# A two-layer attention and retention encoder: pair 14 in seven products in the input projection, pair 15's second low part by ScalarE and an accumulating transfer

## The chip, the cores and the metric

One core of a Trainium2 chip runs the whole program. The metric is the device time of one execution in microseconds (us), the median of several runs. Engines: TensorE (PE; PEld is its weight loading), VectorE (DVE), ScalarE (ACT), GpSimd (POOL), SyncE (SP). SP and POOL issue the transfers (DMAs), each in the order of its own queue.

## The reference

Two layers (DEPTH = 2), 256 tokens, width 4096, all in float32:

```python
for l in range(DEPTH):
    h = rmsnorm(x, norm_w[l])
    proj = h @ w_in[l]                       # 4096 x 11264
    aq, ak, av, ag, rq, rk, rv, rg = jnp.split(proj, SPLIT_POINTS, axis=-1)
    ...                                      # per-head norms, axial rotary
    a_out = silu(ag) * gqa_attention(aq, ak, av)
    r = rmsnorm(bidirectional_retention(rq, rk, rv, log_gf, log_gb), ret_norm[l])
    r_out = silu(rg) * r
    x = x + jnp.concatenate([a_out, r_out], axis=-1) @ w_out[l]   # 4096 x 4096
return rmsnorm(x, final_norm)
```

The two projections are nearly all of the arithmetic. There are 16 attention heads in 4 groups and 8 retention heads in 4 pairs.

## The kernel before

**Phases and blocks.** There are four phases: w_in of layer 0, w_out of layer 0, w_in of layer 1, w_out of layer 1. An input phase has 11 blocks of 2 x 512 columns (BLOCKS, here one "block" is two pieces of the projection, such as `ag` group 0 with `aq` group 0), an output phase four. A block runs over the contraction of 4096 as 16 pairs of two 128-row tiles (NP = 16). So in a block each pair multiplies a 2 x 2 arrangement of tokens and contraction tiles with a 2 x 2 arrangement of contraction tiles and columns. That can be done in eight products of 512 columns (EIGHT_PRODUCTS, line 145) or, with sums of the blocks on both sides, in seven (SEVEN_PRODUCTS, line 134, the scheme of Strassen and Winograd). The two kinds can be mixed in one block, because both add into the same banks of PSUM, M1 to M7. When a block ends, `combining` (line 1690) copies M1 and adds the other banks into two pages, ca and cb.

**Precision.** A float32 operand is split into a high part, rounded to the matmul's fast float32 form (F32R), and a low part, the remainder. One product is three matmuls: high by high, low by high, high by low (`block`, line 1588; the records' names are `M<-whi,x7h` and so on: weights' part, tokens' part; x7 is an operand of a pair in seven products, x8 in eight, xm of a pair that has seven in one kind of phase and eight in the other).

**Weight pages.** Weights come by SP as pages of 512 KB (`wraw`, 128 x 1024 float32, RAWS = 6 slots).
- A pair in eight products has the pages A and B. For each, ScalarE makes the high part (`high`, line 680, a CAST `whi<-wraw`), VectorE the low part (`low`, line 701, `wlo<-wraw,whi`). HIGHS = 4 and LOWS = 3 buffers hold them until PE is done.
- A pair in seven products has four: A, T, B, U. VectorE first makes the sums T (`make_v`, line 623) and U in two halves (`make_u`, `end_u`, lines 634 and 642), each `wsum`. T and U then get a high and a low part like a full page; of B only one half is used (`whb`, `wlb`).
- The page B of some pairs in eight products is **far** (`fars`, line 164): ScalarE makes its high part (`fhi`) and its negated copy (`flo`, `far_parts` and `far_low`, lines 724 and 737), and a transfer by GpSimd's queue adds the weights from memory to that copy (`add`, line 742). VectorE does nothing for it. FAR = 2 buffers hold it, and the work starts FAR_LEAD = 10 us ahead.

Before, SEVEN_IN names the pairs 0, 2, ..., 12 for w_in, SEVEN_OUT 0, 2, ..., 14 for w_out (lines 156 and 157). FAR_IN and FAR_OUT are the odd pairs to 13 (lines 158 and 159). In the border blocks, the last of each input phase and the first of each phase but the very first, `fars` adds pairs in eight products up to BORDER_FAR = 10: before, pairs 14 and 15 in w_in and pair 15 in w_out. In the first block of all, pairs 0, 1, 4 and 5 (DIRECT) are multiplied without splitting, in four passes.

**Order of the work.** The program is written out by a planner: a small simulation with a clock per engine (`Clock`, line 228), a model of the transfers (`Transfers`, line 254) and slots for buffers. At each moment `pick` (line 879) chooses the next instruction of an engine: urgent steps first, then weight operations by their due place in PE's order (`best`, line 763, for VectorE among the next LOOK = 5 that are ready) against steps of tasks. Tasks are what lies between the projections: `in_task` (norms, rotary, gates), `attention_rest` (line 1356) with `attention_pair` (line 1278), `retention_weights`, `retention_pair` and `retention_values` (lines 1480 and 1496). They share PAGES = 8 pages of SBUF with the combining; `running` (line 850) lets a task begin when its `need` of pages is there, at most AT_ONCE = 3 at a time. What they yield is stored to memory, read back and split into operands for the next phase (`Turn`, line 1073; `split_pair`, line 947). All engines' queues run in the planned order.

All VectorE and ScalarE calls pass through line 249, all matmuls through line 1183 (`matmul`), all transfers through line 373 (`dma`); so the rows' lines tell little and their names tell the operation.

Of the kernel before, what the change touches and what calls it, by code (L numbers as in the profile page):

```python
# [12 lines left out]
F32R = mybir.dt.float32r  # L13
# [31 lines left out]
DUE_LEAD = 25.0  # L45
RUSH, SPLIT_LEAD = 2.8, 6.0
# [32 lines left out]
NEED = {"ak": 4, "ag": 3, "rk": 4, "rg": 6}  # L79
# [76 lines left out]
SEVEN_IN = (0,2,4,6,8,10,12)  # L156
SEVEN_OUT = (0, 2, 4, 6, 8, 10, 12, 14)
FAR_IN=(1,3,5,7,9,11,13)
# [69 lines left out]
class Clock:  # L228


    def __init__(self, engine, cost, lap, now):
        self._engine, self._cost, self._lap, self._now = engine, cost, lap, now
        self.until, self._wrote, self.calls = 0.0, None, 0
# [5 lines left out]
    def __getattr__(self, name):  # L239
        call = getattr(self._engine, name)  # L240

        def recorded(out, *args, **kwargs):
            self.until = max(self.until, self._now.t)
            if self._wrote and any(meet(self._wrote, extent(v)) for v in sources(args, kwargs)):
                self.until += self._lap + OWN_PASS
            self.until += self._cost(name, out, args, kwargs) - self._lap
            self._wrote = extent(out)
            self.calls += 1
            return call(out, *args, **kwargs)  # L249

        return recorded
# [96 lines left out]
def hybrid_encoder(  # L348
# [185 lines left out]
    class Weights:  # L534


        def __init__(self):
            self.pages, at = [], 0.0
            for phase in range(2 * DEPTH):
                w = w_out if phase % 2 else w_in  # L540
                for b in range(N_OUT2 if phase % 2 else N_IN):
                    start = (phase, b) == (0, 0)
                    end = (phase, b) == (2 * DEPTH - 1, N_OUT2 - 1)
                    for n, (p, k, uses) in enumerate(pages_in_order(phase, start, end)):
                        g = Page()
                        g.pair, g.kind, g.phase, g.uses = p, k, phase, uses
# [234 lines left out]
    class Lane:  # L781
# [4 lines left out]
        def __init__(self, steps, need=0, own=0, owner=None, after=0.0, hurry=True, due=1e9, start=lambda: True):  # L786
# [62 lines left out]

    def running():  # L850
# [89 lines left out]
    phase_now, need_at = [-1], {}  # L940
    for g in weights.pages:
        if not g.direct:
            need_at.setdefault((g.phase, g.pair), g.at)
    plain, plain_left = {}, list(DIRECT)
# [213 lines left out]
    def split_turned(parts, src):  # L1158

        to = [v.rearrange("p i (m a t) -> p m i a t", m=MT, t=BLK) for v in parts]  # L1160
        v = src.rearrange("p (a m i t) -> p m i a t", a=4, m=MT, t=BLK)
# [11 lines left out]
    def parts_of(name, shape):  # L1173
        return page(shape, name + "h", F32R), page(shape, name + "l", F32R)

# [102 lines left out]
    def attention_pair(g, h, kv, qT, rs, done):  # L1278
# [4 lines left out]
        for e in range(2):  # L1283
            s = (yield from take_bank()).rearrange("p (m k) -> p m k", m=MT)
            for m in range(MT):
                product(s[:, m, :], at(qT, ALL, h + e, slice(m * P, (m + 1) * P)), kT, True, True)
            if h and e:
                drop(2)
# [67 lines left out]
    def attention_rest(L, g):  # L1356
# [86 lines left out]
    def retention_head(wT, v, sg, e, L=None):  # L1443
        o = (yield from take_bank()).rearrange("p (m v) -> p m v", m=MT)
        for m in range(MT):
            for k in range(MT):
                product(
                    o[:, m, :],
                    at(wT, ALL, 2 * e + k, slice(m * P, (m + 1) * P)),
# [3 lines left out]
                )  # L1453
        yield "A"
# [5 lines left out]
        yield 1.0  # L1460
        yield "V"
        if L is not None:
# [5 lines left out]
            return  # L1468
# [9 lines left out]
        free_bank()  # L1478

    def retention_pair(L, i, gacc, vacc):  # L1480
# [4 lines left out]
        for e in range(2):  # L1485
            yield from retention_head(wT, v, gacc, e)
        drop(4)
# [8 lines left out]
    def retention_values(L, i, c, k):  # L1496
# [4 lines left out]
        for e in range(2):  # L1501
            yield from retention_head(wT, v, o, e, L)
        drop(4)
# [420 lines left out]
    def program():  # L1924
        nonlocal sums
        for l, L in enumerate(layers):
            for bi, (one, _) in enumerate(BLOCKS):
# [33 lines left out]
                if one[0] == "rk":  # L1961
                    for i in (2 * one[1], 2 * one[1] + 1):
# [3 lines left out]
                            need=3,  # L1966
                        )
                if one[0] == "ag":
# [4 lines left out]
                        need=6,  # L1973
# [91 lines left out]
```

## Time and profile before

| | us |
|---|---|
| median of 3 runs | 2584.72 (2584.64 to 2585.1) |
| span of the profiled execution, first to last instruction | 2581.7 |
| PE busy | 2565.6 |
| VectorE busy | 2302.2 |
| ScalarE busy | 1914.1 |
| GpSimd busy | 445.3 |

The page gives the profiled execution by its span; a device time of that one execution isn't listed, so the median stands beside it, 3.0 us longer. The granted TensorE clock was 0.998 on average. Busy shares are means over stages; what a stage waits for is read from the views of that stage. A block's end can be found in the trace by ScalarE's copy of M1 (`ca<-M`): the stretches below are cut there, for instance block 6 of layer 0's input phase from 502.2 to 588.1 us.

### The profile page before, as it was taken

Reading aid. Unit: us, or ns where it says so; the run is one execution under the profiler, and the core shown is the slowest. Engines: PE = TensorE matmul, PEld = TensorE weight load, DVE = VectorE, ACT = ScalarE, POOL = GpSimd, SP = SyncE. Lnnn points to the kernel's source line nnn. Section 1 sums busy time; section 2 is a strip of 40 time slices with the busy share of each in tenths; the row PEclk is TensorE's granted clock in tenths of the full one; section 3 lists DMA queues with packets and bytes.
Section 4 is the critical chain, followed back from the end, with each engine's and each line's share of the span. In section 5 each row is a group of like instructions: output and inputs, shape, how many; then the busy total and the mean of one; then the engine's idle time right before and its main releaser. Section 6 shows DMA issues by size and latency. Waiting matters only on the chain.

```text
span 2581.7 us, 34413 instructions
## 1 busy us (share of the span) xinstructions
PE 2565.6 (99%) x11474; PEld 2116.3 (82%) x11474; DVE 2302.2 (89%) x2912; ACT 1914.1 (74%) x2679; POOL 445.3 (17%) x595
## 2 busy tenths in 40 slices
PE   9999999999999999999999999999999999999998
PEld 5888888888888888888888888888888888888886
DVE  7898988998888899888998889989988888998887
ACT  7877776777777688767887776777778777876765
POOL 0022211221221210111212121212212211101110
PEclk9999999999999999999999999999999999999999
DMA  8999989998899899999999999989989998989996
GB/s 303 315 291 289 287 275 289 271 308 266 275 292 284 269 279 251 285 292 291 314 297 283 291 278 279 280 279 285 303 265 284 282 277 264 296 244 283 275 268 227
DMA packets 213107, 727.00 MB, mean 282 GB/s; under 512 B 25520, under 2 KB 32304, under 8 KB 212928
## 3 DMA queue, kind: packets, MB, share of 16 engines
q1 hardware_dynamic: 147616, 521.31, 57.3%
q0 software_dynamic: 65312, 203.49, 34.5%
q8 instruction: 90, 1.47, 0.2%
q14 instruction: 89, 0.73, 0.1%
HBM read 676.46 MB, written 48.23 MB: 281 GB/s over the span
## 4 chain that ended last, share of the span: by engine, by line
PE 95%; DVE 3%; issue 1%; DMA 1%; ACT 0%; POOL 0%; DVEq 0%; POOLq 0%; ACTq 0%
PE M L1183 92%; PE ps L1183 3%; DVE wlo L249 1%; DVE wsum L249 1%; DMA wraw<-in_w_in 0%; DMA flo<-in_w_in 0%; DVE x8l L249 0%; DVE cb L249 0%; PE ps L1022 0%; PE ps L2002 0%; DVE xf L249 0%; DVE x7l L249 0%; DVE ca L249 0%; ACT whi L249 0%; DVE wlb L249 0%
## 5 line engine op out<-in xcount | busy, mean ns | idle before, releaser
L249 ACT CAST whi<-wraw 128x1024 fp32r<-128x1024 f32 x522 | 541.8, 1045 | 176.6 <-PE M L1183 132.8
L249 DVE TENSOR_TENSOR wlo<-wraw,whi 128x1024 fp32r<-128x1024 f32 x522 | 633.1, 1214 | 40.2 <-issue 13.9
L249 DVE TENSOR_TENSOR wlo<-wsum,whi 128x1024 fp32r<-128x1024 f32 x432 | 526.0, 1218 | 132.2 <-PE M L1183 120.0
L249 ACT CAST whi<-wsum 128x1024 fp32r<-128x1024 f32 x432 | 453.4, 1050 | 194.9 <-PE M L1183 139.1
L1183 PE MATMUL M<-whi,x7h 128*128 128x512 f32 x1248 | 487.0, 390 | 0.0
L1183 PE MATMUL M<-whi,x7l 128*128 128x512 f32 x1248 | 485.9, 389 | 0.0
L1183 PE MATMUL M<-whi,x8h 128*128 128x512 f32 x1052 | 409.6, 389 | 0.0
L1183 PE MATMUL M<-whi,x8l 128*128 128x512 f32 x1052 | 409.4, 389 | 0.0
L1183 PE MATMUL M<-wlo,x7h 128*128 128x512 f32 x1248 | 386.1, 390 | 1.7 <-DVE wlo L249 1.5
L1183 PE MATMUL M<-fhi,x8h 128*128 128x512 f32 x836 | 325.7, 390 | 0.0
L1183 PE MATMUL M<-fhi,x8l 128*128 128x512 f32 x836 | 325.4, 389 | 0.0
L1183 PE MATMUL M<-wlo,x8h 128*128 128x512 f32 x1052 | 311.7, 390 | 1.4 <-DVE wlo L249 1.4
L373 POOL DMA_DIRECT2D flo<-in_w_in x156 | 138.4, 887 | 992.0 <-ACT flo L249 878.4
L249 ACT CAST fhi<-wraw 128x1024 fp32r<-128x1024 f32 (+1 forms) x214 | 223.4, 1044 | 110.3 <-PE M L1183 86.3
L249 DVE TENSOR_TENSOR wsum<-wraw 128x1024 f32<-128x1024 f32 x216 | 263.2, 1218 | 15.5 <-DMA wraw<-in_w_in 8.6
L1183 PEld LDWEIGHTS M<-wlo,x7h 128*128 128x128 f32 x1248 | 233.1, 188 | 50.8 <-DVE wlo L249 3.2
L1183 PEld LDWEIGHTS M<-whi,x7l 128*128 128x128 f32 x1248 | 234.4, 188 | 48.9 <-DVE wlo L249 0.2
L1183 PEld LDWEIGHTS M<-whi,x7h 128*128 128x128 f32 x1248 | 234.4, 188 | 48.6 <-issue 0.5
L249 ACT ACTIVATE flo<-fhi 128x1024 fp32r<-128x1024 f32 (+1 forms) x214 | 225.5, 1054 | 9.3 <-PE M L1183 2.4
L1183 PEld LDWEIGHTS M<-wlo,x8h 128*128 128x128 f32 x1052 | 196.8, 188 | 42.2 <-DVE wlo L249 1.9
L1183 PEld LDWEIGHTS M<-whi,x8l 128*128 128x128 f32 x1052 | 197.5, 188 | 41.0
L1183 PEld LDWEIGHTS M<-whi,x8h 128*128 128x128 f32 x1052 | 197.5, 188 | 40.8 <-ACT whi L249 0.3
(280 smaller groups left out, 3779.1 us busy)
## 6 DMA issues: line engine op xcount, KB each, us to landing
wraw<-in_w_in SPq DMA_DIRECT2D x703, 512.0 KB, 5.8
wraw<-in_w_out SPq DMA_DIRECT2D x256, 512.0 KB, 6.2
flo<-in_w_in POOLq DMA_DIRECT2D x156, 512.0 KB, 8.4
flo<-in_w_out POOLq DMA_DIRECT2D x54, 512.0 KB, 8.6
full<-next_dram POOLq DMA_DIRECT2D x18, 512.0 KB, 10.5
p_dram<-room POOLq DMA_DIRECT2D x64, 128.0 KB, 4.0
pT<-p_dram POOLq DMA_DIRECT2D x16, 512.0 KB, 10.8
next_dram<-room POOLq DMA_DIRECT2D x40, 128.0 KB, 5.1
```

What stands on the lines that cost most here:

```text
L249: return call(out, *args, **kwargs)
L373: getattr(nc, name).dma_start(to, src, **kw)
L1183: nc.tensor.matmul(out, a, b, start=start, stop=stop)
```

## The change

In w_in, pair 14 goes from eight to seven products, and page B of pair 15 becomes far in every block (so all eight odd pairs are). Pair 14 is then of the same kind in all phases (no xm operands any more).

The operands of the tasks are split in halves: attention's queries and retention's decayed scores are split two heads (or one head) at a time into one page that holds both parts, instead of all at once into two pages. A task of attention's rest then needs 5 pages (6 before), `rg` tasks 5 (6 before). In `retention_head` the second half is split between the first head's matmuls and its norm.

The planner's rules change too: attention's rest has a due time (REST_LEAD), a start condition by the time left to the next block's border (TAKES in place of `need == 3`), VectorE prefers weight operations that have been ready for SOFT = 0.4 us, the pause after the power function on GpSimd is planned as 1.7 us (1.0), and the clocks also count a lap where an instruction overwrites what the one before it read.

```diff
+REST_LEAD = 20.0
+POOL_REST = 1.7
+SOFT = 0.4
+TAKES = 65.0, 50.0
...
-NEED = {"ak": 4, "ag": 3, "rk": 4, "rg": 6}
+NEED = {"ak": 4, "ag": 3, "rk": 4, "rg": 5}
...
-SEVEN_IN = (0,2,4,6,8,10,12)
+SEVEN_IN = (0, 2, 4, 6, 8, 10, 12, 14)
...
-FAR_IN=(1,3,5,7,9,11,13)
+FAR_IN = (1, 3, 5, 7, 9, 11, 13, 15)
...
-            if self._wrote and any(meet(self._wrote, extent(v)) for v in sources(args, kwargs)):
+            if self._wrote and any(meet(self._wrote, extent(v)) for v in sources(args, kwargs)) or any(meet(v, extent(out)) for v in self._read):
...
-                ops = [o for o in self.ops["V"][:LOOK] if o.ready()]
+                at, ops = now.t, []
+                for rest in (SOFT, 0.0):
+                    now.t = at - rest
+                    ops = ops or [o for o in self.ops["V"][:LOOK] if o.ready()]
+                now.t = at
...
-                if held[0] + v.need - v.own + pledged(v) + (0 if v.own else 2 if v.need == 3 else wanted[0]) + spare() <= PAGES:
+                if held[0] + v.need - v.own + pledged(v) + (0 if v.own else 2 if v.takes > to_border() else wanted[0]) + spare() <= PAGES:
...
+    def parts_in_one(name):
+        v = page([P, 2, 2, SEQ], name, F32R)
+        return v[:, 0], v[:, 1]
...
-        qT = parts_of("aq", [P, 4, SEQ])
-        yield from split_turned(qT, q)
+        done = []
+        qT = parts_in_one("aq")
+        yield from split_turned(qT, q, 0, 2)
+        one = spawn(attention_pair(g, 0, kv, qT, rs, done))
+        qT = parts_in_one("aq")
+        yield from split_turned(qT, q, 2, 2)
         drop()
-        done = []
-        one = spawn(attention_pair(g, 0, kv, qT, rs, done))
...
-        wT = parts_of("wT", [P, 4, SEQ])
-        yield from split(wT, D.rearrange("p (k q) -> p k q", k=4))
+        D = D.rearrange("p (k q) -> p k q", k=4)
+        wT = parts_in_one("wT")
+        yield from split(wT, D[:, :2])
+        return D, wT
...
+        drop(3 if e else 1)
+        wT = None if e else (yield from second(D))
         yield "A"
...
-        yield 1.0
+        yield POOL_REST
...
-                        need=6,
+                        need=5,
+                        takes=TAKES[0],
+                        due=borders[min(bi + 3, N_IN)] - REST_LEAD,
```

## Rows read from the trace of the kernel before

**Rows 1.** The page's busy times: engine, busy us, share of the span, instructions.

```profile
span 2581.7 us, 34413 instructions
PE 2565.6 (99%) x11474; PEld 2116.3 (82%) x11474; DVE 2302.2 (89%) x2912; ACT 1914.1 (74%) x2679; POOL 445.3 (17%) x595
```

**Rows 2.** Three stretches: length; busy PE, PEld, DVE, ACT, POOL; clock, DMA, GB/s.

```profile
0.00:94.40 94.40, 90.92 (x329) 61.17 (x329) 77.14 (x136) 76.93 (x143) 5.20 (x10) 1.00 0.91 307
94.40:2555.30 2460.90, 2459.71 (x11081) 2043.01 (x11082) 2207.91 (x2747) 1827.08 (x2518) 439.01 (x583) 1.00 0.93 282
2555.30:2581.70 26.40, 14.99 (x67) 12.07 (x65) 17.17 (x32) 10.11 (x18) 1.13 (x2) 0.85 0.54 200
```

**Rows 3.** The chain that ended last: start us, length us, what.

```profile
1.49 4.45 PE ps L2002 x10
...
94.37 147.17 PE M L1183 x648
```

**Rows 4.** Whom PE waited for: us in total, times, longest.

```profile
PE M L1183 <- DVE wlo L249: 2.9, 3, 1.4
```

**Rows 5.** Whom VectorE waited for, the first row.

```profile
DVE wlo L249 <- PE M L1183: 132.4, 119, 2.7
```

**Rows 6.** Groups by shape: count, busy us, mean ns of one, idle before, releasers.

```profile
L249 DVE TENSOR_TENSOR wlo<-wraw,whi 128x1024 fp32r<-128x1024 f32 x518 | 630.4, 1219 | 40.2 <-issue 13.9 <-PE M L1183 12.3 <-ACT whi L249 9.3
L249 ACT CAST whi<-wraw 128x1024 fp32r<-128x1024 f32 x518 | 539.3, 1049 | 176.6 <-PE M L1183 132.8 <-DMA wraw<-in_w_in 20.1 <-DMA wraw<-in_w_out 16.8
L249 DVE TENSOR_TENSOR wlo<-wsum,whi 128x1024 fp32r<-128x1024 f32 x432 | 526.0, 1218 | 132.2 <-PE M L1183 120.0 <-ACT whi L249 3.7 <-ACT rkqh L249 3.1
...
L249 DVE TENSOR_TENSOR wsum<-wraw 128x1024 f32<-128x1024 f32 x216 | 263.2, 1218 | 15.5 <-DMA wraw<-in_w_in 8.6 <-DMA wraw<-in_w_out 6.1
...
L249 ACT ACTIVATE flo<-fhi 128x1024 fp32r<-128x1024 f32 x210 | 223.0, 1062 | 9.3 <-PE M L1183 2.4 <-ACT fhi L249 0.4
...
L249 DVE TENSOR_TENSOR wsum<-wsum,wraw 128x512 f32<-128x512 f32 x216 | 147.7, 684 | 1.0
...
L249 DVE TENSOR_TENSOR wlb<-wraw,whb 128x512 fp32r<-128x512 f32 x216 | 147.1, 681 | 19.7 <-ACT whb L249 19.7
L373 POOL DMA_DIRECT2D flo<-in_w_in x156 | 138.4, 887 | 992.0 <-ACT flo L249 878.4 <-ACT xmh L249 56.2 <-PE M L1183 47.7
L249 ACT CAST whb<-wraw 128x512 fp32r<-128x512 f32 x216 | 131.7, 610 | 56.7 <-PE M L1183 45.1 <-issue 11.4 <-ACT whi L249 0.2
```

**Rows 7.** The page's DMA issues: count, KB each, median us to landing.

```profile
flo<-in_w_in POOLq DMA_DIRECT2D x156, 512.0 KB, 8.4
```

**Rows 8.** Stretches, columns as in rows 2: an input phase, two blocks.

```profile
94.40:945.80 851.40, 851.40 (x3861) 708.54 (x3862) 765.59 (x954) 631.18 (x887) 167.44 (x227) 1.00 0.92 283
...
502.20:588.10 85.90, 85.90 (x382) 71.12 (x382) 79.98 (x94) 63.26 (x85) 20.68 (x28) 1.00 0.94 301
...
1201.40:1283.40 82.00, 82.00 (x363) 67.91 (x363) 80.08 (x114) 69.38 (x105) 16.98 (x24) 1.00 0.97 302
```

**Rows 9.** Stretches at the start and the borders, columns as in rows 2.

```profile
60.00:80.00 20.00, 19.86 (x88) 16.24 (x87) 19.93 (x32) 15.74 (x28) 0.85 (x1) 1.00 1.02 324
...
930.00:958.00 28.00, 28.00 (x137) 23.63 (x136) 23.20 (x39) 21.44 (x40) 5.28 (x7) 1.00 0.93 288
...
1320.00:1380.00 60.00, 60.00 (x273) 49.62 (x273) 52.05 (x75) 46.54 (x70) 7.93 (x9) 1.00 0.96 283
```

**Rows 10.** VectorE in order of time: start us, length us, what, idle before.

```profile
88.05 1.23 DVE L249 TENSOR_TENSOR wsum<-wraw 128x1024 f32<-128x1024 f32 x1 [2.78 <-DMA wraw<-in_w_in]
```

More of the change, by code (lines that the diff above doesn't have):

```diff
@@ L243, in recorded @@
             self.until = max(self.until, self._now.t)
-            if self._wrote and any(meet(self._wrote, extent(v)) for v in sources(args, kwargs)):
+            if self._wrote and any(meet(self._wrote, extent(v)) for v in sources(args, kwargs)) or any(meet(v, extent(out)) for v in self._read):
                 self.until += self._lap + OWN_PASS
             self.until += self._cost(name, out, args, kwargs) - self._lap
-            self._wrote = extent(out)
+            self._wrote, self._read = extent(out), [extent(v) for v in sources(args, kwargs)]
             self.calls += 1
@@ L545, in __init__ @@
                         g = Page()
-                        g.pair, g.kind, g.phase, g.uses = p, k, phase, uses
+                        g.pair, g.kind, g.phase, g.block, g.uses = p, k, phase, b, uses
                         g.direct = start and p in DIRECT
@@ L784, in hybrid_encoder, with __init__ @@
         pair = None
-        def __init__(self, steps, need=0, own=0, owner=None, after=0.0, hurry=True, due=1e9, start=lambda: True):
+        def __init__(self, steps, need=0, own=0, owner=None, after=0.0, hurry=True, due=1e9, takes=0.0, start=lambda: True):
+            self.takes = takes
             self.hurry, self.start, self.due = hurry, start, due
@@ L848, in pledge, with to_border @@
         current[0].need = n
+    def to_border():
+        at = weights.place()
+        return next((v - at for v in borders_at if v > at), 1e9)
     def running():
@@ L939, in hybrid_encoder @@
     version = [-1] * NP
-    phase_now, need_at = [-1], {}
+    phase_now, need_at, border = [-1], {}, {}
     for g in weights.pages:
+        border.setdefault((g.phase, g.block), g.at)
         if not g.direct:
             need_at.setdefault((g.phase, g.pair), g.at)
+    borders_at = sorted(border.values())
     plain, plain_left = {}, list(DIRECT)
@@ L1156, in later, with split_turned @@
         return lambda: landed(REST)
-    def split_turned(parts, src):
+    def split_turned(parts, src, h=0, n=4):
         to = [v.rearrange("p i (m a t) -> p m i a t", m=MT, t=BLK) for v in parts]
-        v = src.rearrange("p (a m i t) -> p m i a t", a=4, m=MT, t=BLK)
+        v = src.rearrange("p (a m i t) -> p m i a t", a=4, m=MT, t=BLK)[:, :, h : h + n]
         yield "A"
@@ L1285, in attention_pair @@
             for m in range(MT):
-                product(s[:, m, :], at(qT, ALL, h + e, slice(m * P, (m + 1) * P)), kT, True, True)
-            if h and e:
-                drop(2)
+                product(s[:, m, :], at(qT, ALL, e, slice(m * P, (m + 1) * P)), kT, True, True)
+            if e:
+                drop()
             yield "V"
@@ L1437, in decays, with second, retention_heads, retention_head @@
         yield lambda: landed(W_REST)
-        wT = parts_of("wT", [P, 4, SEQ])
-        yield from split(wT, D.rearrange("p (k q) -> p k q", k=4))
+        D = D.rearrange("p (k q) -> p k q", k=4)
+        wT = parts_in_one("wT")
+        yield from split(wT, D[:, :2])
+        return D, wT
+    def second(D):
+        wT = parts_in_one("wT")
+        yield from split(wT, D[:, 2:])
         drop()
         return wT
-    def retention_head(wT, v, sg, e, L=None):
+    def retention_heads(wT, v, sg, L=None):
+        D, wT = wT
+        for e in range(2):
+            wT = yield from retention_head(wT, v, sg, e, L, D)
+    def retention_head(wT, v, sg, e, L, D):
         o = (yield from take_bank()).rearrange("p (m v) -> p m v", m=MT)
@@ L1484, in retention_pair @@
         wT = yield from decays(i)
-        for e in range(2):
-            yield from retention_head(wT, v, gacc, e)
-        drop(4)
+        yield from retention_heads(wT, v, gacc)
         pledge(2)
@@ L1500, in retention_values @@
         o = page([P, MT, NB], "o")
-        for e in range(2):
-            yield from retention_head(wT, v, o, e, L)
-        drop(4)
+        yield from retention_heads(wT, v, o, L)
         L.pairs = i + 1
@@ L1926, in program @@
         for l, L in enumerate(layers):
+            borders = [border[2 * l, b] for b in range(N_IN)] + [border[2 * l + 1, 0]]
             for bi, (one, _) in enumerate(BLOCKS):
@@ L1966, in program @@
                             need=3,
+                            takes=TAKES[1],
                         )
```

7 lines of the change are left out of this document (4 added, 3 removed).

## The prediction

> **What bounds the kernel now.** I read the page's busy times first: TensorE (PE) is busy for 2565.6 of 2581.7 us, its weight loads for 82%, VectorE for 89%, ScalarE for 74% [rows 1]. Three stretches show where PE's idle 16 us lie: 3.5 before 94.4 us, 11.4 in the last 26.4 us, and 1.2 in the 2460.9 us between [rows 2]. A busy PE need not be a full one, so I turned to the chain of waits: one unbroken piece of it is 648 matmuls in 147.17 us, 0.2271 us each [rows 3], and of that length is every 512-column step. PE's list of waits holds, for the big products, three on VectorE, 2.9 us in all [rows 4]. VectorE, on the other hand, waits 132.4 us, 119 times, for PE to give back a buffer of low parts [rows 5]: it runs ahead, 1.1 us at a time. So from 94.4 us on each matmul that is taken out is worth its 0.227 us, as long as VectorE, now the second busiest, still delivers in time. That is the question.
>
> Here the Trainium skill speaks against it. Its page "Perfetto Trace Analysis", section "Identifying the Most-Contended Engine", says that matmul busy time doesn't tell how full TensorE is and that busy weight loads and the share of peak do; the engine with the highest occupancy is to be relieved first. By that reading PE would have 18% to spare and VectorE's 89% would be the most contended, and the change would load the wrong engine. What it would give is the last rival below. The 0.2271 us per matmul, without a gap over 147 us, doesn't agree with that reading.
>
> **What it removes.** Pair 14 takes seven products instead of eight in the 11 blocks of w_in of both layers. A product is three matmuls (high by high, low by high, high by low). 22 x 3 = 66 matmuls x 0.2271 us = 15.0 us, all on the path that sets the end. PE's matmul records should fall from 11474 to 11408.
>
> **What it adds on VectorE.** As eight products pair 14 needed two low parts, 2 x 1.219 = 2.44 us. As seven it needs low parts of A (1.219), of the two sums T and U (2 x 1.218) and of half of B (0.681), and the sums, 1.218 + 2 x 0.684 [rows 6]: 6.92 us. Difference +4.48. Pair 15's page B loses its low part on VectorE, -1.22. So +3.26 us in each of the 19 blocks where neither pair was far. In the three border blocks (the last block of each input phase, the first of layer 1) both pairs were far already, so that one low part of pair 14 was VectorE's: there it is 6.92 - 1.22 = +5.70, and pair 15 changes nothing. 19 x 3.26 + 3 x 5.70 = 79 us. The split operands cut 24 VectorE operations in two (per attention group two more, per retention pair one more, eight of each); a cut costs the fixed part, 2 x 0.684 - 1.218 = 0.15 us, 3.6 us in all. Pair 14's own operand, twice, some 0.7 us more each (four sums of 128 columns and a wider low part; an estimate from the same slope). Sum: 84 us, VectorE from 2302 to some 2386 us.
>
> **On ScalarE.** Pair 14: three full high parts and a half instead of two, 3 x 1.049 + 0.610 - 2 x 1.049 = +1.66; pair 15: one more pass, the negated copy, +1.06. 19 x 2.72, plus 3 x 0.60 at the borders, plus 24 cuts x 0.17 (2 x 0.610 - 1.049), make about 58 us: 1914 to 1972 us, 77%. Not a bound.
>
> **On GpSimd and the transfers.** Pair 15 far in 19 blocks and pair 14 no longer far in three: 16 more accumulating transfers of 512 KB (156 to 172). Each issue holds GpSimd for 0.887 us [rows 6], 14 us in all. The issue waits for ScalarE's copy, and behind it in GpSimd's queue stand the tasks' stores and fetches and the small power functions of the norms; a fetch then goes out up to one ScalarE pass and one issue later, 1.06 + 0.89 us. The kernel now plans 1.7 instead of 1.0 us for the power function; VectorE does its other work meanwhile, and no matmul of M waits for it. The transfer lands 8.4 us after its issue [rows 7], as those of seven odd pairs per block do now, of which PE's waits show none.
>
> **Is there room inside a phase?** Layer 0's input phase from 94.4 us to its last border takes 851.40 us, with VectorE busy for 765.59 [rows 8]: 85.8 us free in ten blocks. Nine times 3.26, one 5.70 and half of the small items, 2.5, ask for 37.5 us; PE's ten products less shorten the phase by 6.8. Some 41 us stay free. The fullest block, at 502.2, goes from 79.98 us of 85.90 to 83.2 of 85.2, 97.7%. The block of w_out at 1201.4 already runs so: VectorE 80.08 of 82.00 us, also 97.7%, and PE 82.00 of 82.00 [rows 8]. In w_out, moreover, pair 14 has had seven products all along, and pair 15's two low parts come from VectorE outside its first block. I take 0 for the inside of the phases, with an upper end that is the slower rival.
>
> **The start.** Here VectorE sets the pace: 19.93 us of the 20 before 80 us [rows 9]. PE then waits for a low part at 93 us (one of the three waits of [rows 4], at most 1.4 us), after VectorE itself had waited 2.78 us for a page of weights [rows 10]. Block 0 brings VectorE 3.26 + 0.7 - 0.3 = 3.6 us more, the small item less where instructions overlap, and PE comes 0.68 us sooner: 4.3 us if nothing covers it, 4.3 - 2.8 = 1.5 if the wait for the page does. It could even gain: of PE's 3.5 idle us there [rows 2], 2.0 lie behind the first matmul's start at 1.49 [rows 3]. That page is loaded when VectorE releases a slot, so the cover is partial: 2.5 taken.
>
> **The border from layer 0 to layer 1.** From 1320 to 1380 VectorE is busy for 52.05 us of 60 [rows 9]. The border block adds 5.70 + 0.7 and PE comes 0.68 earlier: 7.1 us with no cover, 0 with the 7.95 us that are free, and at best -1.1, the idle time in that block today. ScalarE is busy for 46.54 us there, so not all of that room is where it is wanted. 1.0 taken.
>
> **The two borders into w_out.** The 28 us before 958 leave VectorE 4.8 us [rows 9] for 5.70 + 0.68: up to 1.6 us each, 3.2 together; 0.5 taken.
>
> **The order of the work.** The other edits (0.4 us of rest for VectorE's choices, due times for attention's rest, 5 pages instead of 6, the finer clock) issue nothing of their own; they move the tasks. What hides them is the 41 free us; the cost without that cover is the slower rival.
>
> **Sum.** 15.0 - 2.5 - 1.0 - 0.5 = 11.0 us. The profiled span would go from 2581.7 to 2570.7. The median of the runs shown is 2584.72, 3.0 us beyond that span, for what lies around the first and last instruction; with the same 3.0 it is **2573.7 us**.
>
> **Rivals.**
> - **All of it arrives, or more**: start and borders are covered, as PE's few waits today suggest; against it stands VectorE's 19.93 of 20 us before 80. 2584.7 - 15.0 - (0 to 2) = 2567.7 to 2569.7. Chance 0.06.
> - **The borders eat most of it**: the upper ends together, 4.3 + 7.1 + 3.2 = 14.6, against 15.0: 2584; the stretch from 2579.5 to 2590 is its. For it: VectorE has no free time at the start; against it: 7.95 us are free at the layer's border. Chance 0.13. That pair 14 were not in seven products after all (records still 11474) would end here too, but the table of pairs leaves little doubt: 0.01 within it.
> - **Tasks come late at the border into w_out** (the slower one): the first block of w_out multiplies what attention and retention of the phase have stored. Of VectorE's 279 idle us in the whole run 132 are waits for PE with nothing else ready [rows 5], so tasks may be unable to use such time. Of the 37.5 + 6.8 = 44.3 us that each phase then lacks, what isn't absorbed is waited for by PE before or in blocks 11 and 26 (945.8 and 2224.2 us). It decides from (15.0 - 4.0 + 5.2) / 2 = 8.1 us per border on; with half unabsorbed, 22 us each, 2573.7 + 44 = 2618. Between: 2590 to 2618. For it: the earlier tasks hold pages longer, and a block of 97.7% leaves them little. Against it: 85.8 us free against 44.3, and five pages instead of six let a task begin sooner. Chance 0.15.
> - **VectorE is the bound throughout**, as by the skill's rule: then the time grows by VectorE's 84 us, 2669. Against it: its 2386 us are still 185 short of the span. Chance 0.01.
>
> **How the numbers follow.** Forecast 0.65, rivals 0.06, 0.13, 0.15, 0.01. A measurement of this kernel can tell some 0.2%, 5.2 us, from no change: faster is below 2579.5, and the forecast's own range, 2569.7 to 2579.5, lies there with the first rival: 0.71. Same 0.13, slower 0.16. For 8 in 10 the range goes from 2568.0, the start's gain, to 2592, past the borders' stretch; what is left out is most of the slower rival.
>
> **What would show it.** PE: 11408 records at 0.227 us, idle time 18 to 22 us, the new part of it before 100 us and near 1285 to 1370. VectorE near 2380 us, 92 to 93%; its waits for PE's low buffers clearly under 132 us. 172 accumulating transfers of w_in. Wrong would be: waits of PE for VectorE all through the input phases (room inside the phases misjudged), PE idle for many us around 935 to 1000 and 2210 to 2260 (tasks late), or waits for flo (pair 15's transfer too late).

## The result, and the profile after

The changed kernel takes 2589.05 us in the median of 11 runs (2585.87 to 2593.48); the kernel before, run beside it, 2584.51 (2583.62 to 2586.37). The ratio is 1.0018, 95% interval 1.001 to 1.0026: slower by 0.18%, where 0.4% faster was forecast. The time lies within the range and inside the stretch of the rival that the borders eat the gain. That is luck in good part: the borders into w_out did cost more than was allowed for them, but as much went inside the input phases, and the mechanism was another one at both, as the runs below show. All ratios below are to the kernel before, run beside each changed one.

The page's first lines of the changed kernel, as in [rows 1]:

```profile
span 2584.1 us, 34499 instructions
PE 2555.7 (99%) x11408; PEld 2101.3 (81%) x11408; DVE 2369.4 (92%) x3034; ACT 1959.1 (76%) x2763; POOL 453.6 (18%) x611
```

The work is what was counted. PE has 11408 records, 66 fewer, worth 15.0 us. VectorE has 67 us more (84 were forecast; the single records add up to 82 more, but full-width operations that follow each other begin 1.14 us apart, though each lasts 1.22), ScalarE 45 us more. But PE's idle time went from 16.1 to 28.4 us, +12.3, and its busy time fell by 9.9 only, 5.1 less than the matmuls that went. 12.3 + 5.1 - 15.0 = +2.4 us, the difference of the two spans: 17.4 us were lost where 4.0 had been allowed for. Whom PE waited for (us in total, times, longest), as in [rows 4]:

```profile
PE M L1202 <- DVE wlo L253: 12.4, 17, 2.6
PE M L1202 <- DMA flo<-in_w_in: 2.1, 2, 1.1
PE ps L2037 <- DVE whi L2034: 1.5, 1, 1.5
PE M L1202 <- DVE wlb L253: 0.8, 1, 0.8
```

17 waits for a full low part in place of three, one for the half page's, two for the accumulating transfer in place of none. The 5.1 us more that count as busy go with them: after a wait the first two matmuls come 0.34 us apart, not 0.227, and a pipelined matmul's record of 0.39 us covers the first 0.16 us of any wait behind it.

By place, the same list cut into stretches gives for the changed kernel (before in brackets): start to 100 us 2.1 (1.8); 100 to 980 us 4.8 (0); 980 to 1120 us, out of the border into w_out, 2.7 (0); the layers' border, to 1400 us, 1.2 (1.1); layer 1's input phase 1.5 (0); its border into w_out 2.7 (0); the rest 0.2 (0). VectorE's own waits for PE, 132.4 us in [rows 5], went to 105.5: it runs ahead less often.

The median lies 5.0 us above the profiled span, before 2.8: the profiled run is the fastest of the eleven, and the runs of the changed kernel spread over 7.6 us, those of before over 2.8. A list of waits is always that of one execution, here and below, and where its time lies far from the median this is said.

### The profile page after: what moved, and what is told of

It reads as the page before. It is cut to its first block, busy times and chain, and to the rows that moved or that the text cites. A ratio compares the mean times of both kernels' runs of the same rounds, so it can differ in the third digit from the quotient of the medians.

```text
span 2584.1 us, 34499 instructions
## 1 busy us (share of the span) xinstructions
PE 2555.7 (99%) x11408; PEld 2101.3 (81%) x11408; DVE 2369.4 (92%) x3034; ACT 1959.1 (76%) x2763; POOL 453.6 (18%) x611
## 4 chain that ended last, share of the span: by engine, by line
PE 85%; DVE 8%; issue 3%; DMA 2%; ACT 1%; POOL 0%; SPq 0%; DVEq 0%; POOLq 0%; ACTq 0%
PE M L1202 82%; DVE wlo L253 3%; PE ps L1202 3%; DVE wsum L253 2%; DMA flo<-in_w_in 1%; DVE x8l L253 1%; DVE cb L253 1%; DMA wraw<-in_w_in 1%; DVE wlb L253 0%; DVE ca L253 0%; DVE x7l L253 0%; DVE xf L253 0%; ACT whi L253 0%; DMA pT<-p_dram 0%; DMA full<-in_xT 0%
## 5 line engine op out<-in xcount | busy, mean ns | idle before, releaser
L253 DVE TENSOR_TENSOR wlo<-wsum,whi 128x1024 fp32r<-128x1024 f32 x476 | 579.7, 1218 | 114.7 <-PE M L1202 105.5
L253 ACT CAST whi<-wsum 128x1024 fp32r<-128x1024 f32 x476 | 499.5, 1049 | 208.5 <-PE M L1202 106.6
L253 ACT CAST whi<-wraw 128x1024 fp32r<-128x1024 f32 (+1 forms) x484 | 498.6, 1045 | 137.0 <-PE M L1202 80.8
L253 DVE TENSOR_TENSOR wlo<-wraw,whi 128x1024 fp32r<-128x1024 f32 (+1 forms) x484 | 585.9, 1213 | 5.6 <-ACT whi L253 4.1
L1202 PE MATMUL M<-whi,x7h 128*128 128x512 f32 x1428 | 557.0, 390 | 0.0
L1202 PE MATMUL M<-whi,x7l 128*128 128x512 f32 x1428 | 555.9, 389 | 0.0
L1202 PE MATMUL M<-wlo,x7h 128*128 128x512 f32 x1428 | 443.3, 391 | 7.6 <-DVE wlo L253 7.6
L1202 PEld LDWEIGHTS M<-whi,x7l 128*128 128x128 f32 x1428 | 268.1, 188 | 55.8 <-issue 0.5
L1202 PEld LDWEIGHTS M<-whi,x7h 128*128 128x128 f32 x1428 | 268.2, 188 | 55.5 <-ACT full L253 0.2
L1202 PE MATMUL M<-flo,x8h 128*128 128x512 f32 x912 | 257.7, 390 | 2.1 <-DMA flo<-in_w_in 2.1
```

Source lines behind the costliest of these rows:

```text
L1202: nc.tensor.matmul(out, a, b, start=start, stop=stop)
```

## The experiments

Four theories. **A**: VectorE's added work comes late, and PE waits for low parts. **B**: the split operands and the planner's new rules cost the time, not the pairs. **C**: GpSimd's queue and the accumulating transfers. **D**, formed after the first four runs: what decides is the order that the planner writes, whatever the load; a new order, by any edit, loses several us.

### One part of the change alone

**Only the edits of the order** (the tables of before):

```diff
-SEVEN_IN = (0, 2, 4, 6, 8, 10, 12, 14)
+SEVEN_IN = (0, 2, 4, 6, 8, 10, 12)
-FAR_IN = (1, 3, 5, 7, 9, 11, 13, 15)
+FAR_IN = (1, 3, 5, 7, 9, 11, 13)
```

> The changed kernel with pair 14 back in eight products and pair 15 not far in w_in: only the split operands and the planner's rules are left. The changed kernel's 66 matmuls less are worth 15.0 us, yet its PE loses some 17 us more in waits than before. Theory A (VectorE's added work comes late in bursts): without that work PE's waits are again near those of before, 2582 to 2588 us. Rival B (the other edits of the order cost it): most of the 17 us of waits stay while the 15 us of matmuls come back, 2597 to 2603 us. Rival C (pair 15's transfers and GpSimd's queue): as A, near 2585.

Measured: 2589.76 us, ratio 1.0021 (1.0012 to 1.003). PE's waits in it, with VectorE at 2307 us, 5 more than before:

```profile
PE M L1202 <- DVE wlo L253: 5.7, 4, 2.0
PE M L1202 <- DMA flo<-in_w_in: 1.8, 2, 1.3
```

So the edits alone cost some 5.5 us, and the two tables on top of them bring nothing: 15.0 us of matmuls go and the median stays. The time lies in the range of neither A nor B.

**Only the tables** (the kernel before, SEVEN_IN and FAR_IN of the changed one):

```diff
-SEVEN_IN = (0,2,4,6,8,10,12)
+SEVEN_IN = (0, 2, 4, 6, 8, 10, 12, 14)
-FAR_IN=(1,3,5,7,9,11,13)
+FAR_IN = (1, 3, 5, 7, 9, 11, 13, 15)
```

> The kernel before with the two tables changed alone: pair 14 in seven products and pair 15 far in w_in; no split operands, none of the planner's new rules. The matmuls are 15.0 us less. Theory A (VectorE's added 80 us come late): PE waits as in the changed kernel, 2587 to 2592 us. Theory B (the other edits of the order cost some 6 us, as they did alone): without them 2580 to 2585. Theory D (the order that the planner writes is what decides, and any edit shifts PE's waits by several us either way): no sum of the parts holds; here 2590 to 2602, since the edits were made to make room for these tables.

Measured: 2610.45 us, ratio 1.0101 (1.0087 to 1.0115).

```profile
PE M L1183 <- DVE wlo L249: 10.8, 14, 1.8
PE M L1183 <- DVE cb L249: 6.2, 3, 3.1
PE M L1183 <- DMA flo<-in_w_in: 5.3, 2, 3.8
PE M L1183 <- ACT ca L249: 4.4, 3, 1.6
```

Two rows are new: PE waits for `ca` and `cb`, the combining of the block before, which gives it back the banks. The combining starts when two pages are free; that tasks hold them longer here is argued from the code, not read from a row. With these tables, then, the split operands and the rules are worth 21 us; with the old tables they cost 5.5. The parts don't add up, and the time lies above the ranges of all three theories.

**Pair 14 in seven products without pair 15 far, and the reverse.**

```diff
-FAR_IN = (1, 3, 5, 7, 9, 11, 13, 15)
+FAR_IN = (1, 3, 5, 7, 9, 11, 13)
```

> The changed kernel, pair 14 in seven products, but pair 15's page B is not far except at the borders: VectorE has 1.22 us more per block (16 to 19 blocks, about 23 us in all), ScalarE 1.06 less, 16 accumulating transfers fewer. A: PE's waits for VectorE grow, 2592 to 2605 us. B: no change against the changed kernel, about 2589. C: PE's waits on flo go and the time falls to 2580 to 2586.

Measured: 2587.83 us, ratio 1.0014 (1.0006 to 1.0023). In its profile VectorE is busy for 2390.2 us, PE waits 15.4 us for low parts (12.4 in the changed kernel) and 0.2 for flo (2.1). A's direction in the waits, C's in the flo row; but this profile is of the slowest of its eleven runs, that of the changed kernel of the fastest. In the time the difference is inside the intervals: what pair 15's transfer is worth here can't be told from nothing.

```diff
-SEVEN_IN = (0, 2, 4, 6, 8, 10, 12, 14)
+SEVEN_IN = (0, 2, 4, 6, 8, 10, 12)
```

> The changed kernel with pair 14 back in eight products, pair 15 still far in every block: VectorE has 1.22 us less per block than with the order edits alone, the transfers stay. A: PE's waits are those of before or fewer, 2581 to 2587 us. B: as the order edits alone, 2597 to 2603. C: the transfers bring PE waits on flo and the time is 3 to 8 us above the order edits alone.

Measured: 2591.83 us, ratio 1.0032 (1.002 to 1.0044), with VectorE at 2288.0 us, 14 less than before. A alone would have it at least as fast as before; PE waits 6.4 us for low parts, 1.9 for flo and 3.1 for `aq`, the queries' split part. It is 2.1 us above the edits alone, where C expected 3 to 8. Less work on VectorE than before, and slower: the first hint at D.

### VectorE's work taken away

**Without pair 14's sums** (T and U are split from the raw page):

```diff
-                    self.op("V", a, SUM_LEAD, self.v_ready, self.make_v)
-                    self.op("V", a, SUM_LEAD - 0.01, self.u_ready, self.make_u)
-                    self.op("V", a, SUM_LEAD - 0.02, lambda g: g.u_part is not None, self.end_u)
+                    if not self.plain14(g):
+                        self.op("V", a, SUM_LEAD, self.v_ready, self.make_v)
+                        self.op("V", a, SUM_LEAD - 0.01, self.u_ready, self.make_u)
+                        self.op("V", a, SUM_LEAD - 0.02, lambda g: g.u_part is not None, self.end_u)
...
```

> The changed kernel, but in w_in VectorE doesn't make pair 14's two sums (2.58 us per block, 57 us in all); its pages T and U are split from the raw page A instead, so that part of the computation is left out, and all matmuls, transfers and ScalarE passes stay. A: with VectorE's added work mostly gone PE's waits fall back to about those of before, and the 15 us of matmuls show: 2569 to 2576 us. B: the waits stay, 2585 to 2590. C: the waits on flo stay, 2583 to 2588.

Measured: 2579.89 us, ratio 0.9984 (0.9975 to 0.9993). VectorE 2325.1 us, 44 less; PE's waits for low parts 6.8 us in place of 13.2. Half of A's effect in the waits, and a time between the ranges of A and C. But the planner wrote a new order here too.

**Without three of the combining's additions in w_in**:

```diff
-                to = {"M3": cb[:, 0, :], "M2": ca[:, 0, :], "M4": ca[:, 1, :]}[b]
-                ve.tensor_add(to, to, acc[b])
+                if phase_now[0] % 2:
+                    to = {"M3": cb[:, 0, :], "M2": ca[:, 0, :], "M4": ca[:, 1, :]}[b]
+                    ve.tensor_add(to, to, acc[b])
```

> The changed kernel without three of the additions of the combining at the end of each of the 22 w_in blocks (M2, M3 and M4 are not added: that part of the computation is left out): VectorE has 66 x 0.68 = 45 us less, taken away just at the blocks' borders where most of PE's new waits stand; everything else is issued as before. A: PE's waits for VectorE shrink by half or more, 2572 to 2580 us. B: by little, 2584 to 2588. D: the order is written anew and PE's waits don't follow VectorE's load; the time can even grow, 2590 to 2608.

Measured: 2603.09 us, ratio 1.0077 (1.0064 to 1.0089): VectorE is relieved at the ends of the w_in blocks, and the kernel loses 14 us.

```profile
PE 2560.0 (98%) x11408; PEld 2102.4 (81%) x11408; DVE 2340.1 (90%) x2971; ACT 1958.0 (75%) x2763; POOL 453.4 (17%) x611
```

PE's waits in it:

```profile
PE M L1202 <- DVE wlo L253: 11.2, 14, 2.6
PE M L1202 <- DMA flo<-in_w_in: 7.6, 2, 5.9
PE M L1202 <- ACT ca L253: 5.0, 3, 1.7
```

29 us less on VectorE, no fewer waits for low parts (a further row has 3.6 us for half pages), and 7.6 us of waiting for two transfers. The profile is of the slowest of its five runs. It doesn't decide on A, because the order is new: by the two traces about two thirds of VectorE's operations keep their sequence. What differs is that order, and where transfers stand in it. An experiment on load must therefore leave the order alone.

**The same order, VectorE lighter.** The planner counts each operation in full, and only the instruction that goes out is narrower (32 columns, for operations that write over one of their inputs):

```diff
+CUT = 32
...
             self.calls += 1
+            if self._lap == 0.083 and name.startswith(("tensor_", "scalar_")) and count(out) >= 256 and out.shape[-1] > CUT and any(
+                extent(v) == extent(out) and tuple(v.shape) == tuple(out.shape) for v in sources(args, kwargs)
+            ):
+                args = [v[..., :CUT] if hasattr(v, "shape") and tuple(v.shape) == tuple(out.shape) else v for v in args]
+                out = out[..., :CUT]
             return call(out, *args, **kwargs)
```

> The changed kernel with its order of instructions untouched, but VectorE's in-place additions and multiplications (the combining's later additions, the tasks' rotary, gate and decay products) work on 32 columns of each row only, while the planner counts them in full: about 100 us of VectorE's time go, that part of the computation is left out, and nothing else moves. A (in this order PE waits because VectorE is late): PE's waits for VectorE fall from 13 us to at most 4, and the time to 2572 to 2578 us. D (the order itself, whatever VectorE's load): the waits stay, 2584 to 2590. C (transfers): only the waits on flo stay, 2 us.

Measured: 2579.18 us, ratio 0.9983 (0.9974 to 0.9992), 9.9 us less than the changed kernel, between A's range and D's. In the two traces VectorE, ScalarE and GpSimd run the same operations in the same sequence, one by one, so this run differs by the load alone; that only the order decides, whatever the load, falls.

The page's line of busy times, and then PE's waits:

```profile
PE 2552.9 (99%) x11408; PEld 2102.6 (82%) x11408; DVE 2239.4 (87%) x3034; ACT 1958.1 (76%) x2763; POOL 451.9 (18%) x611
```

```profile
PE M L1208 <- DVE wlo L259: 8.2, 12, 2.0
PE M L1208 <- DMA flo<-in_w_in: 1.6, 2, 1.3
```

So in the changed kernel's own order 130 us of VectorE's load are worth 9.9 us. 1.0 us of that lies behind the last matmul, where the end of the kernel is shorter (10.6 us for 11.6). The change added only 67 us, and what those alone cost no run tells: 9.9 us is an upper end for them. And at 63 us below its load before, PE still waits 9.3 us for low parts, 2.9 before. That rest isn't the sum of VectorE's work; the order is what is left for it.

### The order alone

**The kernel before with one planned pause of 1.7 us**, and **the changed kernel with it at 1.0** and **with other constants**:

```diff
-        yield 1.0
+        yield 1.7
```

> The kernel before, with the one pause after the retention heads' power function planned as 1.7 us instead of 1.0: no work is added or removed, no table is changed. A and C: within 2 us of before, 2582 to 2587. D (the order of before is one in which PE hardly waits, and any edit of the order loses some of that): slower by 2 to 8 us, 2586 to 2592.

Measured: 2583.55 us, ratio 0.9998 (0.9989 to 1.0007). D in its strong form, that any edit of the order costs, falls. The edit is a mild one: by the two traces nine in ten of VectorE's operations keep their sequence.

```diff
-POOL_REST = 1.7
+POOL_REST = 1.0
```

> The changed kernel with the pause after the power function planned as 1.0 us again (1.7 in the changed one): no instruction is added or removed, sixteen steps of the retention heads may come 0.7 us sooner, and VectorE may wait for GpSimd there, up to 11 us in all. A: the work is the same, so 2587 to 2591. B: a part of the 6 us comes back, 2583 to 2588. D: a shift of 3 us or more either way although no work changes; 2582 to 2586 is my guess.

Measured: 2588.37 us (2580.79 to 2590.72), ratio 1.0015 (1.0006 to 1.0024): no shift in the median, within 1 us of the changed kernel. But the spread is 9.9 us, and the profile, of one of the slowest runs (2590.64), has 5.6 us of waits for flo.

```diff
-POOL_REST = 1.7
-SOFT = 0.4
+POOL_REST = 1.0
+SOFT = 0.3
...
-RUSH, SPLIT_LEAD = 2.8, 6.0
+RUSH, SPLIT_LEAD = 2.9, 6.0
...
-HIGH_LEAD = 3.2
-SUM_LEAD = 2.0
+HIGH_LEAD = 3.6
+SUM_LEAD = 2.5
```

> The changed kernel with five of the planner's constants moved by little (pause 1.0, rest 0.3, sums due 2.5 and high parts 3.6 us ahead, hurry 2.9): the same work in another order. A: the work is the same, so 2586 to 2591 us. D: the order is worth several us; an order in which PE waits less may keep most of the 15 us, 2576 to 2584.

Measured: 2587.83 us, ratio 1.001 (1.0001 to 1.0019). Another order, the same time: these five moves don't find a way out.

**What the order does at a border.** A clear place to read it is where block 11, the first of w_out, ends. VectorE's rows of the changed kernel (start us, length us, what):

```profile
1041.18 1.22 DVE L253 TENSOR_TENSOR wlo<-wraw,whi 128x1024 fp32r<-128x1024 f32 x1
1042.32 0.68 DVE L253 TENSOR_TENSOR cb<-ca,M 128x512 f32<-128x512 f32 x1
1043.03 0.69 DVE L253 TENSOR_TENSOR ca<-cb,M 128x512 f32<-128x512 f32 x1
1043.63 1.22 DVE L253 TENSOR_TENSOR wsum<-wraw 128x1024 f32<-128x1024 f32 x1
1044.77 0.68 DVE L253 TENSOR_TENSOR cb<-cb,M 128x512 f32<-128x512 f32 x1
1045.37 0.68 DVE L253 TENSOR_TENSOR cb<-ca,M 128x512 f32<-128x512 f32 x1
...
1047.87 0.69 DVE L253 TENSOR_TENSOR ca<-ca,M 128x512 f32<-128x512 f32 x1
1048.47 0.69 DVE L253 TENSOR_TENSOR wsum<-wsum,wraw 128x512 f32<-128x512 f32 x1
1049.07 2.35 DVE L253 TENSOR_TENSOR wlo<-wraw,whi 128x1024 fp32r<-128x1024 f32 x2
```

And of the kernel before at the same border:

```profile
1041.63 0.69 DVE L249 TENSOR_TENSOR cb<-ca,M 128x512 f32<-128x512 f32 x1 [0.61 <-PE M L1183]
...
1044.16 1.22 DVE L249 TENSOR_TENSOR wlo<-wraw,whi 128x1024 fp32r<-128x1024 f32 x1
1045.30 0.68 DVE L249 TENSOR_TENSOR cb<-ca,M 128x512 f32<-128x512 f32 x1
...
1047.09 1.22 DVE L249 TENSOR_TENSOR wlo<-wraw,whi 128x1024 fp32r<-128x1024 f32 x1
1048.22 0.68 DVE L249 TENSOR_TENSOR ca<-ca,M 128x512 f32<-128x512 f32 x1
```

Before, a low part stands among the combining's additions every 3 us. After, two low parts stand ahead of them, and then none begins until 1049.07, 7.9 us after the last: all seven additions (two of them left out above) and a page's sums come first. PE waits 1.6 us there, and 1.7 at the same place of layer 1. The rest of the 2.7 us per border are three waits of 0.3 to 0.4 us ahead of it, from 1014 on. The sum of VectorE's work is not the difference: in the 92 us up to this point it is the same. The stretches of before, then of after (length; busy PE, PEld, DVE, ACT, POOL):

```profile
958.00:1038.00 80.00, 79.91 (x360) 65.86 (x359) 78.74 (x118) 67.74 (x99) 7.67 (x9) 1.00 0.91 256
1038.00:1050.00 12.00, 12.00 (x54) 9.94 (x53) 11.27 (x15) 8.42 (x10) 0.72 (x1) 1.00 0.71 200
```

```profile
958.00:1038.00 80.00, 79.35 (x356) 64.89 (x355) 78.31 (x125) 68.09 (x105) 9.67 (x12) 1.00 0.85 254
1038.00:1050.00 12.00, 10.32 (x45) 7.84 (x43) 11.94 (x17) 8.28 (x10) 1.06 (x1) 1.00 0.63 182
```

90.0 us before and 90.3 after. But VectorE is nearly full in both, and it runs later after: from 972.5 to the wait it never stood idle for more than 0.1 us, while before it had three such spells, 0.61 us the last of them, at 1041.63. Late work and order are told apart by the lightened kernel, which keeps the order. There VectorE stands idle at this border, twice for 0.57 us, at the combining's additions, which wait for PE's last products of their banks, while the low part that PE will need stands behind them in the queue:

```profile
1043.73 0.19 DVE L259 TENSOR_TENSOR ca<-ca,M 128x32 f32<-128x32 f32 x1 [0.57 <-PE M L1208]
1043.83 0.69 DVE L259 TENSOR_TENSOR wsum<-wraw,wsum 128x512 f32<-128x512 f32 x1
1045.09 0.19 DVE L259 TENSOR_TENSOR ca<-ca,M 128x32 f32<-128x32 f32 x1 [0.57 <-PE M L1208]
1045.19 0.69 DVE L259 TENSOR_TENSOR wsum<-wsum,wraw 128x512 f32<-128x512 f32 x1
1045.80 2.35 DVE L259 TENSOR_TENSOR wlo<-wraw,whi 128x1024 fp32r<-128x1024 f32 x2
```

PE still waits 1.1 us there. So of the 1.6 us the order holds 1.1 even at that load, and late work the other 0.5. The same sequence, with a wait of 1.7 us, stands in the kernel with the tables alone; with the edits alone PE waits 2.0 us at this border, in another sequence.

Inside the input phases it is otherwise. The longest wait of all, 2.6 us at 175, comes after a stretch of only 3.8 us without a low part:

```profile
172.59 1.22 DVE L253 TENSOR_TENSOR wlo<-wsum,whi 128x1024 fp32r<-128x1024 f32 x1
...
176.39 1.22 DVE L253 TENSOR_TENSOR wlo<-wraw,whi 128x1024 fp32r<-128x1024 f32 x1
```

VectorE had not stood idle for more than 0.1 us since 149.5; in the lightened kernel it has, and PE waits 2.0 us there. And two stretches without a low part, 8.1 us up to 523.6 and 7.8 up to 1801.2, bring no wait at all. How long the queue holds none is thus not enough to tell a wait; what PE still has in its buffers when the stretch begins should count too, which no row here shows.

### GpSimd's queue

Both flo waits of the changed kernel come from one place, the same in both layers. GpSimd's rows around the first (ScalarE's copy for the transfer was ready at 546.8; PE waits until the transfer, issued at 555.05, lands at 564.58):

```profile
544.80 0.91 POOL L377 DMA_DIRECT2D rkq<-rk_dram  x1
552.47 0.88 POOL L377 DMA_DIRECT2D rkq<-rq_dram  x1 [6.76 <-DVE wsum L253]
553.37 1.72 POOL L512 TENSOR_TENSOR rs<-rs,half 128x8 f32<-128x8 f32 x1
555.05 1.82 POOL L377 DMA_DIRECT2D flo<-in_w_in  x2
```

The two rkq issues stand one behind the other in the code, and nothing but the first lies between them in the queue; yet the second begins 6.8 us after the first ended. The row names VectorE, but most gaps of this kind end with no releaser at all; among GpSimd's waits of the kernel before they make up nearly all of one row (us in total, times, longest):

```profile
POOL rkq L373 <- issue: 60.1, 8, 10.3
```

Six of the eight gaps there are in it, 9.1 to 10.3 us each; the other two (7.0 and 7.8) go by PE's name. In the changed kernel the eight are 4.7 to 9.1 us. What they end with can be read from the landings: in all eight pairs, of both kernels, the second issue begins 0.4 us after the first fetch has landed (here at 552.06), though the program doesn't make it wait for that: no semaphore of the first fetch is among those that the second one waits for. The row of the first fetch in the changed kernel (count, KB each, median us from issue to landing):

```profile
rkq<-rk_dram POOLq DMA_DIRECT2D x8, 256.0 KB, 7.1
```

Elsewhere the queue doesn't do this: behind the second fetch the next instruction follows at once, and the two transfers at 555.05 go out back to back. A fetch of rkq moves 256 KB in pieces of 256 bytes, 1024 of them; that the queue waits for room for their descriptors would fit, but no row shows it. Behind the second fetch stand the power function and the flo of a pair, and PE has to wait when that pair is due. With the pause of 1.0 us the gaps at the same two places were 7.2 and 7.9 us and PE's waits 2.4 and 3.2, here 6.8 and 6.5 and the waits 1.1 and 1.0. The test takes the kernel with the pause of 1.0 us and puts the fetch on SP's queue:

```diff
-POOL_REST = 1.7
+POOL_REST = 1.0
...
-        landed = dma("gpsimd", raw[:, k], src[:, :, 2 * BLK * (i % 2) : 2 * BLK * (i % 2 + 1)])
+        landed = dma("sync", raw[:, k], src[:, :, 2 * BLK * (i % 2) : 2 * BLK * (i % 2 + 1)])
```

> As the run with the pause of 1.0 us, but the retention operands' fetch (rkq, in the traces the one GpSimd issue after which the next waits 5 to 9 us for nothing that the profile shows) goes through SP's queue. That run had 5.6 us of PE waits on flo. C (GpSimd's queue held by rkq delays flo): these waits go, and the time falls from 2588.4 to 2581 to 2585 us. D: another order, a shift either way; SP's weights behind the fetch may come late and show as waits for wraw: 2586 to 2592.

Measured: 2583.18 us (2580.91 to 2585.02), ratio 0.9994 (0.9985 to 1.0003), against 2588.37 with the fetch on GpSimd's queue: 5.2 us, as C had it. The planner's order changes a little with it (nine in ten of VectorE's operations keep their sequence); the two pauses above changed it as little and moved the time by less than 1 us. In its profile the flo row is gone, PE's waits for low parts are the old ones (12.1 us for 11.1), and the gap is gone too:

```profile
547.66 2.04 POOL L512 TENSOR_TENSOR rs<-rs,half 128x8 f32<-128x8 f32 x1 [1.10 <-DVE rs L253]
549.66 0.90 POOL L377 DMA_DIRECT2D flo<-in_w_in  x1
```

The pages also count the packets. Those of GpSimd's queue (q0) and of SP's (q1), with the fetch on GpSimd's queue, then on SP's:

```profile
q1 hardware_dynamic: 147616, 521.31, 56.2%
q0 software_dynamic: 67616, 211.88, 35.8%
```

```profile
q1 hardware_dynamic: 164256, 525.50, 57.3%
q0 software_dynamic: 66336, 207.69, 35.3%
```

The same 4.19 MB are 1280 packets on GpSimd's queue, 80 for each of the 16 fetches, and 16640 on SP's, 1040 for each. On GpSimd's queue, then, the pieces of 256 bytes go many to a packet, and still it stands.

The spread fell from 9.9 to 4.1 us. Of the kernels here that compute all of the reference with the new tables it is the only one whose time can't be told from that of before; the others are slower.

**Both relieved**, VectorE lighter in that kernel's order:

> Both relieved at once: the kernel whose retention fetch goes through SP's queue (2583.2 us), in its own order of instructions, with VectorE's in-place additions and multiplications on 32 columns only (that part of the computation is left out). If VectorE's lateness (A) and the held GpSimd queue (C) are two separate causes, their gains add: 2583.2 less the 8 to 10 us that the same lightening gave the changed kernel, 2573 to 2576 us, with no PE wait on flo left. If they are one and the same (VectorE late makes ScalarE and so flo late), it stays at 2577 to 2580, as the lightened kernel alone. D: 2580 to 2586.

The edit is that of the lightened kernel, on this one. Measured: 2576.63 us (2572.8 to 2576.96), ratio 0.9969 (0.9957 to 0.9981).

```profile
PE M L1208 <- DVE wlo L259: 6.7, 8, 2.0
PE M L1208 <- DVE wlb L259: 2.5, 1, 2.5
```

No flo row. By the ratios, relieving VectorE brings 0.25% here and 0.35% in the changed kernel, and the fetch brings 0.14% beside a light VectorE and 0.21% without. The time lies between what was expected of two separate causes and of one, and such differences are inside the intervals: there are two causes, and whether they overlap isn't told. Together the two undo 0.49% of the 0.76% that lie between the changed kernel (1.0018) and the full gain (1 - 15.0 / 2584.5 = 0.9942). The rest, 0.27% or 7 us, is waiting that remains with VectorE 63 us below its load before (10.0 us for the big products in this profile). Of it 1.1 us stand at the end of block 11 and 1.1 at the same place of layer 1, where the order holds them; for the others, 2.5 us at the start and 2.0 at 178 the longest, no run isolates the cause.

## Why the prediction was wrong

- **What it removes**: right, 66 records, 15.0 us.
- **VectorE's and ScalarE's added work**: right in its parts, a quarter too high (67 and 45 us for 84 and 58), because lengths of single rows were added where operations overlap: added up so, the trace after gives 82 and 57.
- **"Is there room inside a phase? ... I take 0"**: the step that failed first. It compared sums over blocks of 80 us. PE takes a page's low part every few us from three buffers, and it waits when VectorE's queue brings the next one too late: at 175 us, where VectorE had worked for 25 us without a pause of more than 0.1 us, even if 40 us are free elsewhere in the phase. Inside the input phases the waits for low parts and for flo came to 6.3 us. The block at 1201.4, taken as the proof that 97.7% does no harm, showed one good order, not a law: block 12 of the changed kernel has a PE wait of 1.6 us with VectorE at 72.78 of 84.30 us, 86%. It comes at the block's start, where 12 us were full.
- **The start** (2.5) and **the layers' border** (1.0): 0.3 and 0.1 us were measured. The cover that was argued from [rows 10] was nearly used up at the start: VectorE's wait for the page went from 2.78 to 0.35 us.
- **The two borders into w_out** (0.5, at most 3.2): 5.4 us of waits. The mechanism was sought before 958 us, in VectorE's free time; it sat 90 us later, in the order of the combining against the low parts, at the same load over the 92 us. Lighter work in the same order left 2.9 of the 5.4.
- **GpSimd and the transfers**: priced at up to 1.95 us of delay for a task's fetch, and nothing for PE. Turned round, it was the tasks' fetch that delayed flo: 5.2 us by the run on SP's queue. The gaps between the rkq issues, 7.0 to 10.3 us, were in the trace of before, and the prediction passed over them; a flo stood directly behind three of the eight there, and PE waited for none.
- **The order of the work**: "issue nothing of their own" was true, and yet the edits alone cost 5.5 us; with the tables they save 21. Edits of a planned order have no price of their own; they have one with each load.
- **The rivals**: tasks late at the border into w_out was not what happened: PE has no wait from 930 to 1000 us, and those that follow are for low parts. The rule of the most contended engine, the last rival, would have given 2669; measured are 4.5 us, in its direction. In "Perfetto Trace Analysis", section "Identifying the Most-Contended Engine", the Trainium skill has the engine with the highest occupancy be relieved first. The lightened run, which took 130 us off VectorE alone and gained 9.9, bears it out for this kernel to that extent; PE's 0.227 us a matmul between its waits still stands.

## What to carry to other kernels

When an engine is fed by an in-order queue through a few buffers, don't judge an added load by its free time over a stage. Look for the stretches in which that queue holds none of the feeder's steps, and for those in which it never pauses; read its rows at each border where urgent work of another kind meets it. An added transfer on a shared queue can be held by the slowest issue ahead of it, so list the gaps of that queue, those without a releaser too, before calling it free. And to learn what a load costs in a program whose order is planned, keep the order fixed and shorten the instructions; leaving instructions out wrote a new order here, and with less work it was 14 us slower.

## What the hardware showed that was not expected

- GpSimd's queue stood still for 4.7 to 10.3 us between two fetches in pieces of 256 bytes, until the first had landed: 0.4 us after it the second issue began, in all eight pairs of the kernel before and of the changed one, mostly with nothing in the profile that released it. On SP's queue the same second fetch took 0.53 to 5.12 us to issue, median 2.57, and that profile has no PE wait for flo or for a page of weights.
- Such a fetch was 80 packets on GpSimd's queue and 1040 on SP's, for the same 256 KB.
- The spread of a kernel's runs went with its flo waits: 9.9 us with 5.6 us of them in the profile, 4.1 us with none, on the same tables and constants. That the flo waits vary from run to run and make the spread is likely but not shown, since only one execution of each is profiled.
